# A decoder trunk on one core: down projections with the high and low activations side by side in one 512-column matmul

## The chip, the core and the metric

The kernel runs on one core of one Trainium2 chip. The metric is the device time of one execution in microseconds, as the median of several runs. The engines of the core have the profile's names here: PE is TensorE (matmuls, with PEld for the loads of its stationary weights), DVE is VectorE, ACT is ScalarE, POOL is GpSimd and SP is SyncE, which issues the transfers of the weights.

## What is computed

The reference is a decoder trunk of two layers on 256 tokens of 1024 features. Layer 0 mixes tokens with a recurrent block, layer 1 with sparse attention. A squared-ReLU MLP of width 4096 follows each mixer. The change touches the second product of that MLP, `w_down`, and the residual addition behind it.

```python
def _sq_relu_mlp(h, w_up, w_down):
    u = jax.nn.relu(h @ w_up)
    return (u * u) @ w_down

for i in range(DEPTH):
    h = _rmsnorm(x, norm_mix[i])
    x = x + mixer(h)
    h = _rmsnorm(x, norm_ffn[i])
    x = x + _sq_relu_mlp(h, mlp_w_up[i], mlp_w_down[i])
return _rmsnorm(x, norm_final)
```

## The kernel before

Everything is held transposed: a tile has 128 features on the partitions and the 256 tokens (S) along its free dimension. The residual stream `xt` is eight such chunks, and an output chunk m of a product is one accumulation in a PSUM bank, 128 partitions by 256 tokens, a half of the bank's 512 float32 columns.

The products need more precision than one pass of TensorE's reduced float32 (`F32R`) gives. So each operand is split into a high part, rounded to that format, and a low part, the difference. A product is then three matmuls for each 128-row slice k: high weights by high activations, high weights by low activations, low weights by high activations. `mm3` (lines 317 to 320) issues them in this order, and each brings a load of its own stationary weight tile, 128 by 128:

```python
pe.matmul(ps, wh, xh, start=start, stop=False)
pe.matmul(ps, wh, xl, start=False, stop=False)
pe.matmul(ps, wl, xh, start=False, stop=stop)
```

`start` clears the bank, and the matmuls behind it add to it until `stop`. The high weights come from ACT (line 278, tile `whi`), the low ones from DVE (line 287, `wlo`), both from a raw tile that SP loads (line 264). There are seven buffers of each, and `tick` (line 300) keeps the splitting up to six pieces ahead of the product that uses them. One piece is 128 by 1024: eight slices k.

The MLP is the function `mlp` (line 766). It first runs 32 up projections, whose results are squared and split on DVE and ACT (lines 778 to 785) into 32 tiles `uhl`. Such a tile is 512 columns wide, the high part `uh` in its first half and the low part `ul` in its second:

```python
uhl = [up.tile([P, 2 * S], F32R, name="uhl", tag="uhl", bufs=NF) for _ in range(NF)]
uh, ul = [x[:, :S] for x in uhl], [x[:, S:] for x in uhl]
zrot = rotation(3, 4, 5, 0, 1, 2)
```

Then come the down projections (lines 797 to 817): eight output chunks m, each of four pieces j with eight slices k, so 32 slices and 96 matmuls a chunk. The banks go round a rotation of six. At the end of a chunk `residual` (line 521) adds the bank to `xt` on DVE, and an epilogue follows: in layer 0 the scaled copies for the next mixer (`chunk_h`, `hhl`) and the squares for the norm, in layer 1 the scaling by the final norm. The eighth chunk of layer 1 is another case (`seeded`): the residual is put into the bank by two identity matmuls ahead of it, and `finish` takes the result from the bank.

What runs in which order in the MLP is the order of the code. The two sections around it (recurrent block and attention) are ordered by a planner, which is given a duration and the needs of each piece of work; its tables are not changed.

Of the kernel before, what the change touches and what calls it, by code (L numbers as in the profile page):

```python
# [20 lines left out]
S = 256  # L21
D = 1024
KC = D // P
NF = 32
# [195 lines left out]
def trunk_kernel(ctx: ExitStack, tc: tile.TileContext, x_in, vec_in, const_in, w2_in, wts, out):  # L220
    nc = tc.nc
    ctx.enter_context(tc.manual_schedule())
    pe, dve, act, pool = nc.tensor, nc.vector, nc.scalar, nc.gpsimd
# [12 lines left out]
    def rotation(*ids):  # L236
        while True:
            for i in ids:
                yield bank(i)
# [52 lines left out]
    def later(fn):  # L292
        deferred.append(fn)

    def flush():
        todo, deferred[:] = deferred[:], []
        for fn in todo:
            fn()

    def tick(lo=None, hi=None, n=1):  # L300
        for i in range(max(n, 1)):
            more = n and state["split"] - state["get"] < LOOK
            if more:
                split_lo(lo)
            if i == 0:
                flush()
            if more:
                split_hi(hi)

    def get(name, idx):  # L310
        i = state["get"]
        assert order[i] == (name, idx), (order[i], name, idx)
        state["get"] += 1
        assert state["lo"] > i
        return hi_t[i % NSPL], lo_t[i % NSPL]

    def mm3(ps, wh, wl, xh, xl, start, stop):
        pe.matmul(ps, wh, xh, start=start, stop=False)  # L318
        pe.matmul(ps, wh, xl, start=False, stop=False)  # L319
        pe.matmul(ps, wl, xh, start=False, stop=stop)  # L320

    def diff(o, a, h):
        return lambda e: e.tensor_tensor(o, a, h.bitcast(F32), op=OP.subtract)  # L323
# [9 lines left out]
    class Section:  # L333
# [55 lines left out]
        def proj(self, name, idx, b, t, step, xs=None, xk=None):  # L389
            wh, wl, wk = self.weight(name, idx, t)  # L390
            z = self.bank((name, idx), b, zcols)
            xs, xk = xs or [(hh[:, k], hl[:, k]) for k in range(KC)], xk or hkey
            for i in range(0, 4, self.join):
                ks = range(2 * i, 2 * (i + self.join))

                def run(e, ks=ks):
                    for k in ks:
                        w = slice(k * P, (k + 1) * P)
                        mm3(z(), wh[:, w], wl[:, w], xs[k][0], xs[k][1], k == 0, k == KC - 1)
                self.add("pe", 0.68 * self.join, run, r=wk + list(xk[ks.start:ks.stop]), w=[("ps", b)], t=t + i * step)  # L400
            return z, ("ps", b)
# [119 lines left out]
    def residual(z, m):  # L521
        dve.tensor_tensor(xt[:, m], xt[:, m], z, op=OP.add)  # L522


    with ExitStack() as ph:
# [45 lines left out]
        for k in range(KC):  # L571
# [6 lines left out]
                w=[("hh", k)], t=t)  # L578
# [3 lines left out]
        for q in range(4):  # L582
            for i in range(NFINE):
                w = slice(256 * q, 256 * q + 256)
# [6 lines left out]
        for a, b, n in ((0, 2, 2), (0, 1, 1), (4, 6, 2), (4, 5, 1), (0, 4, 1)):  # L591
            add("dve", 0.07 + 0.267 * n, lambda e, a=a, b=b, n=n: e.tensor_tensor(
                x2[:, a:a + n], x2[:, a:a + n], x2[:, b:b + n], op=OP.add), r=[("x2", b + i) for i in range(n)],
                w=[("x2", a + i) for i in range(n)], t=4 + a / 4)
# [43 lines left out]
        zb = {"n": 0}  # L638
# [5 lines left out]
        def conv(m, t):  # L644
            b = nextbank()
            if m < NFINE:
                wh, wl, _ = sec.weight("in", 8 + m, t)
                z, zk = sec.bank(("in", 8 + m), b, zcols), ("ps", b)
                for k in range(KC):
                    def run(e, k=k):  # L650
                        w = slice(k * P, (k + 1) * P)
                        mm3(z(), wh[:, w], wl[:, w], hh[:, k], hl[:, k], k == 0, k == KC - 1)
                        if m == 0 and k == 1:
                            keep_warm(8)
                    add("pe", 0.323 + 0.9 * (m == 0 and k == 1), run, r=[("hi0", m, k // 2), ("lo0", m, k // 2), ("hi", m), ("lo", m), hkey[k]],
                        w=[zk], t=m * 0.33 + k * NI * PJ / 2 if m < NI else t + k * PJ / 2)
            else:
                z, zk = sec.proj("in", 8 + m, b, t, PJ)
            t += 4 * PJ
            x, xk = xps[m % 3], ("xp", m % 3)  # L660
            bk = ("xb", m)
            add("dve", 0.34, lambda e: e.tensor_tensor(x[:, 3:], z(), rs, op=OP.mult), r=[zk, "rs"], w=[xk], t=t)
            add("act", 0.49, lambda e: e.activation(xb[m], x[:, 3:], AF.Identity, bias=col(V_CB, m), scale=cw(3, m)),
                r=[xk], w=[bk], t=t)
            for i in range(3):
                add("dve", 0.4, lambda e, i=i: e.scalar_tensor_tensor(xb[m], x[:, i:i + S], cw(i, m), xb[m], op0=OP.mult,
                                                                      op1=OP.add), r=[xk], w=[bk], t=t)
# [82 lines left out]
        for m in range(8):  # L750
            wh, wl, wk = sec.weight("out", m, to + 2.65 * m)
            b = nextbank()
            z = sec.bank(("out", m), b, zcols)
            for i in range(4):
                def run(e, i=i, z=z, wh=wh, wl=wl):
                    for k in (2 * i, 2 * i + 1):
                        w = slice(k * P, (k + 1) * P)
                        mm3(z(), wh[:, w], wl[:, w], xbh[k], xbl[k], k == 0, k == KC - 1)
                add("pe", 0.68, run, r=wk + pk[2 * i] + pk[2 * i + 1], w=[("ps", b)], t=to + 2.65 * m + i * PJ)
            t = to + 2.65 * (m + 1)  # L760
            add("dve", 0.34, lambda e, z=z, m=m: residual(z(), m), r=[("ps", b)], w=[("xt", m)], t=t)
            sec.norm(m, V_GF, t)
# [3 lines left out]
    def mlp(layer, epilogue, first, last=None):  # L766
        with ExitStack() as ph:
            up = ph.enter_context(tc.tile_pool(name="up%d" % layer, bufs=1, side="right"))
            tmp = ph.enter_context(tc.tile_pool(name="mtmp%d" % layer, bufs=2))
            if last:  # L770
                xh, xl, ir = (tmp.tile([P, n], F32R, name=a, bufs=1) for a, n in (("xh", S), ("xl", S), ("ir", P)))
# [4 lines that stand above are left out]
            def up_post(m, z):  # L776
                t = tmp.tile([P, S], F32, name="t", tag="t")
                dve.scalar_tensor_tensor(t, z, 0.0, rs, op0=OP.max, op1=OP.mult)  # L778
                flush()
                if m >= len(first) - 1:  # L780
                    tick(n=2 if m < 16 else 1)
                u = tmp.tile([P, S], F32, name="u", tag="u")
                act.activation(u, t, AF.Square)  # L783
                act.activation(uh[m], t, AF.Square)  # L784
                later(lambda: dve.tensor_tensor(ul[m], u, uh[m].bitcast(F32), op=OP.subtract))  # L785

            for m in range(NF):
                if m >= len(first):
                    z = next(zrot)[:, :S]
                    wh, wl = get("up%d" % layer, m)  # L790
                    for k in range(KC):
                        w = slice(k * P, (k + 1) * P)
                        mm3(z, wh[:, w], wl[:, w], hh[:, k], hl[:, k], k == 0, k == KC - 1)
                else:
                    z = first[m]()
                up_post(m, z)
            for m in range(8):
                z = next(zrot)[:, :S]
                seeded = last is not None and m == 7
                if last and m == 6:  # L800
                    act.copy(ir, ident)
                    act.copy(xh, xt[:, 7])
                    diff(xl, xt[:, 7], xh)(dve)
                if seeded:
                    pe.matmul(z, ir, xh, start=True, stop=False)
                    pe.matmul(z, ir, xl, start=False, stop=False)
                for j in range(4):
                    wh, wl = get("dn%d" % layer, m * 4 + j)
                    for k in range(8):
                        w, i = slice(k * P, (k + 1) * P), j * 8 + k  # L810
                        mm3(z, wh[:, w], wl[:, w], uh[i], ul[i], i == 0 and not seeded, i == NF - 1)
                    if j == 3 and seeded:
                        last(z)
                    elif j == 3:
                        residual(z, m)
                        epilogue(m)
                    tick()

    def to_mix(m):
        chunk_h(m, V_GM, m < KC - 1)  # L820
        chunk_stats(m)

    mlp(0, to_mix, up0)


    with ExitStack() as ph:
# [36 lines left out]
        for i in range(2):  # L863
            o = offs[-1] + (4 + i) * P * 1024
            add("sp", 1.5, lambda e, i=i, o=o: e.dma_start(w1[i], wts[o:o + P * 1024].rearrange("(p n) -> p n", p=P)),
                w=[("w1", i), "loads"] + w1k, t=-12, lag=2.0)
# [544 lines left out]
```

## Time and profile before

| | |
|---|---|
| median of 3 runs | 568.36 us (568.14 to 568.47) |
| profiled execution, span from first to last instruction | 566.4 us |
| up projections of layer 0 end, down projections of layer 0 begin | 174.3 us |
| first matmul of the attention section | 261.5 us |
| down projections of layer 1, first seven chunks | 470.8 to 546.9 us |
| eighth chunk, to its last matmul | to 558.0 us |
| VectorE busy from 174.3 to 261.5 us | 48.97 us |
| ScalarE busy from 174.3 to 261.5 us | 34.56 us |
| PEclk from 174.3 to 261.5 us | 1.00 |

A row of the groups gives source line, engine, operation, the tiles written and read, the shapes, the count, the busy time and the mean duration of one. Behind the second bar stands how long the engine was idle just ahead of it, and what ended that. A row of the timeline gives the start in us, the duration in us, the engine, the line and the operation. Matmuls overlap: the duration of one reaches from its start through the array to the bank, and the next one starts long before that. What a matmul costs in a stream is the interval between two starts.

### The profile page before, as it was taken

How to read it: one execution, taken by the hardware profiler on the slowest of the kernel's cores; microseconds unless marked ns; L12 is line 12 of the kernel's file. 1: busy time of each engine (PE TensorE's matmuls, PEld its weight loads, DVE VectorE, ACT ScalarE, POOL GpSimd, SP SyncE). 2: the span in 40 equal slices, each digit the busy share in tenths (PEclk: the TensorE clock that was granted, in tenths of full speed). 3: DMA queues.
4: the chain of work that ended last, by engine and by line, in shares of the span. 5: the costliest groups of instructions: out<-in, count | busy, mean ns of one | idle time of the engine just before them, and what ended most of it. 6: DMA issues, size and time to landing. Idle time of an engine off the chain costs nothing.

```text
span 566.4 us, 12406 instructions
## 1 busy us (share of the span) xinstructions
PE 559.3 (99%) x4902; PEld 552.9 (98%) x4902; DVE 407.6 (72%) x873; ACT 343.9 (61%) x670; POOL 40.1 (7%) x55
## 2 busy tenths in 40 slices
PE   9999999999999999999999999999999999999995
PEld 9989999999999999999999999999999999999995
DVE  6899989776676565466839999999767775563532
ACT  7699675866564443354647999875855664443421
POOL 1000000000000121131000000000000000222310
PEclk9999999999999999999999999999999999999998
DMA  8936467566667456555765431264766667566402
GB/s 319 407 91 220 117 219 247 176 204 192 188 192 249 155 189 217 190 181 175 276 188 166 140 99 57 75 224 138 221 200 192 196 200 233 154 202 221 132 1 74
DMA packets 33225, 103.66 MB, mean 183 GB/s; under 512 B 3856, under 2 KB 8080, under 8 KB 33168
## 3 DMA queue, kind: packets, MB, share of 16 engines
q1 hardware_dynamic: 32624, 102.42, 56.1%
q8 instruction: 38, 0.62, 0.5%
q10 hardware_dynamic: 544, 0.46, 0.2%
q14 instruction: 19, 0.16, 0.1%
HBM read 99.23 MB, written 1.05 MB: 177 GB/s over the span
## 4 chain that ended last, share of the span: by engine, by line
PE 99%; DVE 0%; ACT 0%; DVEq 0%; POOL 0%; issue 0%; POOLq 0%
PE bank L318 28%; PE bank L319 28%; PE bank L320 28%; PE bank L1177 3%; PE bank L686 2%; PE bank L1159 2%; PE bank L1105 1%; PE bank L1106 1%; PE bank L567 1%; PE bank L1012 1%; PE bank L1013 1%; PE bank L1014 1%; PE bank L953 1%; DVE xg L1295 0%; PE bank L1287 0%; DVEq L1406 0%
## 5 line engine op out<-in xcount | busy, mean ns | idle before, releaser
L318 PE MATMUL bank<-hhl,whi 128*128 128x256 f32 x768 | 213.1, 278 | 0.0
L319 PE MATMUL bank<-hhl,whi 128*128 128x256 f32 x768 | 212.4, 277 | 0.0
L320 PE MATMUL bank<-hhl,wlo 128*128 128x256 f32 x768 | 212.3, 276 | 0.0
L318 PEld LDWEIGHTS bank<-hhl,whi 128*128 128x128 f32 x768 | 144.5, 188 | 0.1
L287 DVE TENSOR_TENSOR wlo<-raw,whi 128x1024 fp32r<-128x1024 f32 x115 | 143.2, 1266 | 1.9 <-ACT whi L278 1.9
L319 PEld LDWEIGHTS bank<-hhl,whi 128*128 128x128 f32 x768 | 144.5, 188 | 0.1
L320 PEld LDWEIGHTS bank<-hhl,wlo 128*128 128x128 f32 x768 | 144.4, 188 | 0.0
L319 PE MATMUL bank<-uhl,whi 128*128 128x256 f32 x512 | 141.4, 276 | 0.0
L320 PE MATMUL bank<-uhl,wlo 128*128 128x256 f32 x512 | 141.3, 276 | 0.0
L318 PE MATMUL bank<-uhl,whi 128*128 128x256 f32 x512 | 141.3, 276 | 0.0
L278 ACT CAST whi<-raw 128x1024 fp32r<-128x1024 f32 x116 | 118.1, 1039 | 23.1 <-issue 18.8
L318 PEld LDWEIGHTS bank<-uhl,whi 128*128 128x128 f32 x512 | 96.1, 188 | 0.0
L320 PEld LDWEIGHTS bank<-uhl,wlo 128*128 128x128 f32 x512 | 96.1, 188 | 0.0
L319 PEld LDWEIGHTS bank<-uhl,whi 128*128 128x128 f32 x512 | 96.1, 188 | 0.0
L323 DVE TENSOR_TENSOR wlo<-raw,whi 128x1024 fp32r<-128x1024 f32 (+2 forms) x72 | 77.1, 1089 | 2.9 <-ACT whi L326 2.8
L326 ACT CAST whi<-raw 128x1024 fp32r<-128x1024 f32 (+2 forms) x64 | 61.2, 969 | 16.8 <-PE bank L319 7.8
L522 DVE TENSOR_TENSOR xt<-xt,bank 128x256 f32<-128x256 f32 x39 | 15.9, 417 | 74.8 <-PE bank L320 74.5
L783 ACT ACTIVATE u<-t 128x256 f32<-128x256 f32 x64 | 26.7, 418 | 58.6 <-DVE t L778 57.2
L778 DVE SCALAR_TENSOR_TENSOR t<-bank,rstd 128x256 f32<-128x256 f32 x64 | 26.9, 423 | 41.0 <-PE bank L320 40.7
L1119 ACT ACTIVATE pt<-pt,mx 128x128 f32<-128x128 f32 (+1 forms) x64 | 28.6, 450 | 1.8 <-DVE mx L1116 1.4
L785 DVE TENSOR_TENSOR uhl<-u,uhl 128x256 fp32r<-128x256 f32 x64 | 26.6, 416 | 3.0 <-ACT uhl L784 3.0
L498 ACT ACTIVATE hhl<-xt,vec 128x256 fp32r<-128x256 f32 x8 | 4.1, 510 | 39.4 <-DVE xt L522 39.4
(202 smaller groups left out, 732.6 us busy)
## 6 DMA issues: line engine op xcount, KB each, us to landing
raw<-in_dram SPq DMA_DIRECT2D x171, 512.0 KB, 4.4
raw<-in_dram SPq DMA_DIRECT2D x4, 560.0 KB, 4.6
gw<-in_dram SPq DMA_DIRECT2D x4, 512.0 KB, 8.9
raw<-in_dram SPq DMA_DIRECT2D x6, 256.0 KB, 4.9
y<-in_dram SPq DMA_DIRECT2D x2, 512.0 KB, 7.4
pT<-in_dram SPq DMA_DIRECT2D x2, 512.0 KB, 5.4
xt<-in_dram SPq DMA_DIRECT2D x3, 256.0 KB, 4.9
kl<-tl SPq DMA_DIRECT2D x8, 64.0 KB, 4.0
```

What stands on the lines that cost most here:

```text
L278: (act.copy if eng is None else eng.tensor_copy)(hi_t[i % NSPL][:, :n], raw_of(i)[:, :n])
L287: (eng or dve).tensor_tensor(lo[:, :n], raw_of(i)[:, :n], hi[:, :n].bitcast(F32), op=OP.subtract)
L318: pe.matmul(ps, wh, xh, start=start, stop=False)
L319: pe.matmul(ps, wh, xl, start=False, stop=False)
L320: pe.matmul(ps, wl, xh, start=False, stop=stop)
L323: return lambda e: e.tensor_tensor(o, a, h.bitcast(F32), op=OP.subtract)
L326: return lambda e: (e.copy if e is act else e.tensor_copy)(o, a)
L778: dve.scalar_tensor_tensor(t, z, 0.0, rs, op0=OP.max, op1=OP.mult)
L783: act.activation(u, t, AF.Square)
L785: later(lambda: dve.tensor_tensor(ul[m], u, uh[m].bitcast(F32), op=OP.subtract))
L1119: add("act", (0.39, 0.49)[qc], lambda e, row=row, j=j: e.activation(row, row, AF.Exp, bias=mx[:, j:j + 1], scale=-1.0, accum_out=sm[:, j:j ...
L1177: two = lambda c, w, y, **k: [e.matmul(o()[own_(hf), c0 + c.start:c0 + c.stop], w(hf), y(hf), **k) for hf in range(2)]
```

## The change

A new helper `mm2` takes the place of `mm3` in all down projections but the eighth chunk of layer 1. It moves the whole `uhl` tile, 512 columns, against one load of the high weights, and writes a whole bank: the first half gets high by high, the second half high by low. Then it moves the high activations against the low weights into the second half. So there are two accumulations side by side in one bank, and `residual` is called twice at a chunk's end, once for each half.

```diff
+    def mm2(ps, wh, wl, xhl, start, stop):
+        pe.matmul(ps, wh, xhl, start=start, stop=False)
+        pe.matmul(ps[:, S:], wl, xhl[:, :S], start=False, stop=stop)
...
             for m in range(8):
-                z = next(zrot)[:, :S]
+                zf = next(zrot)
+                z, zb = zf[:, :S], zf[:, S:]
...
-                        mm3(z, wh[:, w], wl[:, w], uh[i], ul[i], i == 0 and not seeded, i == NF - 1)
+                        if seeded:
+                            mm3(z, wh[:, w], wl[:, w], uh[i], ul[i], False, i == NF - 1)
+                        else:
+                            mm2(zf, wh[:, w], wl[:, w], uhl[i], i == 0, i == NF - 1)
                     if j == 3 and seeded:
                         last(z)
                     elif j == 3:
                         residual(z, m)
+                        residual(zb, m)
                         epilogue(m)
```

Four lines are added ahead of everything else, so a line of the old kernel behind 320 has a number higher by four or more in the new one; the two matmuls of `mm2` are lines 323 and 324, and `residual` is line 526.

In PE's order, where layer 0's down projections begin (`bank` is the PSUM bank, `hhl` the last up projection's activations, `whi` and `wlo` the weight pieces), before:

```order
L320 MATMUL bank_2275<-hhl,wlo_96 128x256
L318 MATMUL bank_2309<-uhl,whi_83 128x256
L319 MATMUL bank_2309<-uhl,whi_83 128x256
L320 MATMUL bank_2309<-uhl,wlo_90 128x256
L318 MATMUL bank_2309<-uhl,whi_83 128x256
```

and in the changed kernel, from the same place:

```order
L320 MATMUL bank_2275<-hhl,wlo_96 128x256
L323 MATMUL bank_2309<-uhl,whi_83 128x512
L324 MATMUL bank_2309<-uhl,wlo_90 128x256
L323 MATMUL bank_2309<-uhl,whi_83 128x512
L324 MATMUL bank_2309<-uhl,wlo_90 128x256
```

Of the three matmuls of a slice, two have become one of twice the width; over the kernel PE has 480 matmuls less.

In DVE's order, at the end of layer 0's first chunk (`raw` is a loaded piece, `xt` the residual stream), before:

```order
L287 TENSOR_TENSOR wlo_90<-raw_79,whi_83 128x1024
L522 TENSOR_TENSOR xt<-xt,bank_2309 128x256
L287 TENSOR_TENSOR wlo_91<-raw_80,whi_84 128x1024
L501 SCALAR_TENSOR_TENSOR hhl<-xt,vec,hhl 128x256
L287 TENSOR_TENSOR wlo_92<-raw_81,whi_85 128x1024
```

and in the changed kernel:

```order
L287 TENSOR_TENSOR wlo_90<-raw_79,whi_83 128x1024
L526 TENSOR_TENSOR xt<-xt,bank_2309 128x256 x2
L287 TENSOR_TENSOR wlo_91<-raw_80,whi_84 128x1024
L505 SCALAR_TENSOR_TENSOR hhl<-xt,vec,hhl 128x256
L287 TENSOR_TENSOR wlo_92<-raw_81,whi_85 128x1024
```

One addition has become two in a row; all else on DVE, and all of ACT, POOL and SP, stands as before.

The end of layer 0's last chunk is followed by the first projections of the attention section, which use the scaled copies `hhl` slice by slice. In PE's order (here with the buffers' numbers and the engines waited for) the last slice comes late in that sequence, behind parts of three chunks, in the kernel before:

```order
L320 MATMUL bank2_3317<-hhl_106,wlo6_96 128x256
L318 MATMUL bank0_3269<-hhl_106,whi4_87 128x256
L319 MATMUL bank0_3269<-hhl_106,whi4_87 128x256
L320 MATMUL bank0_3269<-hhl_106,wlo4_94 128x256
L318 MATMUL bank0_3269<-hhl_106,whi4_87 128x256 [waits Activation_49]
L319 MATMUL bank0_3269<-hhl_106,whi4_87 128x256 [waits DVE_49]
```

Nothing moved there: the changed kernel has the same rows at this place, 45 matmuls behind the section's first in both.

## The prediction

> **What bounds the kernel now.** I read the page first: the shares of the engines, then the chain that ended last, then the costliest groups.
>
> ```profile
> span 566.4 us, 12406 instructions
> PE 559.3 (99%) x4902; PEld 552.9 (98%) x4902; DVE 407.6 (72%) x873; ACT 343.9 (61%) x670; POOL 40.1 (7%) x55
> PE 99%; DVE 0%; ACT 0%; DVEq 0%; POOL 0%; issue 0%; POOLq 0%
> L318 PE MATMUL bank<-uhl,whi 128*128 128x256 f32 x512 | 141.3, 276 | 0.0
> ```
>
> The chain is TensorE from end to end, and PE never waits before the down projections' matmuls (idle 0.0). So the time is the sum of the intervals from one matmul's start to the next. The 276 ns of a group's row is no such interval: it is a latency, and 512 of them three times over would be far more than the two stages last. The interval comes from starts, so I asked for the instructions on the tile uhl, once for layer 0's down projections and once for the first seven chunks of layer 1's (the eighth is not changed).
>
> ```profile
> L318 PE MATMUL bank<-uhl,whi x256: 276/276/280, 174.3 to 261.2; 128*128 128x256 f32 x128
> L318 PE MATMUL bank<-uhl,whi x224: 276/276/281, 470.8 to 546.6; 128*128 128x256 f32 x112
> ```
>
> Between the first and the last L318 lie 255 steps in 86.9 us (340.8 ns) and 223 steps in 75.8 us (339.9 ns). A step is the three matmuls of one 128-row slice k, so **one step costs 340.4 ns**, 113.5 ns a matmul, and the change touches 256 + 224 = 480 steps, 163.4 us of the span. One ns on a step is 0.48 us.
>
> **The change part by part.** Removed: in each of 480 steps the second load of the same high weight tile and one matmul instruction. Kept: the columns that move, 3 x 256 before, 512 + 256 now. So nothing is computed less; what can be won or lost is what a matmul costs beside its columns. No matmul of 512 columns stands in the trace, and its price decides everything. I look for rows that separate a part for each matmul from a part for each column.
>
> First, the stream as it is, in the timeline near the end of layer 1's seventh chunk:
>
> ```profile
> 545.14 0.28 PE L320 MATMUL bank<-uhl,wlo 128*128 128x256 f32 x1
> 545.25 0.28 PE L318 MATMUL bank<-uhl,whi 128*128 128x256 f32 x1
> ...
> 546.84 0.28 PE L320 MATMUL bank<-uhl,wlo 128*128 128x256 f32 x1
> ```
>
> From 545.14 to 546.84 there are 15 matmuls: 113.3 ns each. But the same matmuls, with the same tiles, also run at another pace. At the start of layer 0's down projections:
>
> ```profile
> 174.56 0.28 PE L320 MATMUL bank<-uhl,wlo 128*128 128x256 f32 x1
> 174.68 0.28 PE L318 MATMUL bank<-uhl,whi 128*128 128x256 f32 x1
> ...
> 177.06 0.28 PE L320 MATMUL bank<-uhl,wlo 128*128 128x256 f32 x1
> ```
>
> Here 21 matmuls take 2.50 us, 119 ns each. So 256 columns have **two paces**, 113.3 and about 118 to 119, and the fast one is what the kernel has nearly all the time. Now the only long stretch in which reduced-precision matmuls of different lengths follow each other, three of 304 columns and three of 256 in turn (the value projections, also with a weight load each):
>
> ```profile
> 280.12 0.30 PE L1012 MATMUL bank<-whi,hhl 128*128 128x304 f32 x1
> 280.26 0.30 PE L1013 MATMUL bank<-wlo,hhl 128*128 128x304 f32 x1
> 280.39 0.30 PE L1014 MATMUL bank<-whi,hhl 128*128 128x304 f32 x1
> 280.53 0.28 PE L1012 MATMUL bank<-whi,hhl 128*128 128x256 f32 x1
> 280.65 0.28 PE L1013 MATMUL bank<-wlo,hhl 128*128 128x256 f32 x1
> 280.77 0.28 PE L1014 MATMUL bank<-whi,hhl 128*128 128x256 f32 x1
> 280.89 0.30 PE L1012 MATMUL bank<-whi,hhl 128*128 128x304 f32 x1
> ...
> 283.20 0.30 PE L1012 MATMUL bank<-whi,hhl 128*128 128x304 f32 x1
> ```
>
> Four rounds take 3.08 us, 770 ns a round of 1680 columns; in the first round three matmuls of 256 take 0.36 us and three of 304 take 0.41. I put 118 ns on the 256 and so 770/3 - 118 = 138.7 on the 304. The fast pace does not come back in these four rounds: a length that differs from the one before keeps the stream in the slow pace. Third, what a column costs at most when nothing else does:
>
> ```profile
> L686 PE MATMUL bank<-xb,gw x64: 378/379/380, 29.5 to 43.8; 128*128 128x256 f32 x64
> 29.48 13.11 PE L686 MATMUL bank<-xb,gw 128*128 128x256 f32 x60
> ```
>
> These are full-precision matmuls (32 calls in the code, 64 instructions). Sixty in a row last 13.11 us, of which the last one's latency is 0.38, so 59 intervals of 215.8 ns. If that is two passes over 256 columns, a column costs at most 215.8/512 = 0.42 ns.
>
> **The sum.** A matmul of 512 columns is a 304 with 208 more: 138.7 + 208 x 0.42 = 226 ns. The 256 behind it I take at the slow pace, 118, since it follows a longer one as in the value projections. A step is then 344 ns against 340.4, +3.6 ns, times 480 = **+1.7 us**. In words: two matmuls that each carry about 11 ns beside their columns against three that carry 113.3 - 256 x 0.42 = 6. The ends of the range for the 512: 215.8 (the row that lasts nearest to it, without any extra) and 512 x 770/1680 = 234.7 (all of a round's time put on columns). For the 256: 113.3 and 119. I choose values near the 304, since it is the longest single-pass matmul that the trace has.
>
> **A rule against this forecast.** The row first: 138.7 ns for 304 columns, with a load of the next weights beside it. The Trainium skill, page "TensorE: Matmul & The Clock Gate", section "Step-by-step: what each phase is for", says that the next weights come through a read port of their own and take no bandwidth from the matmul that runs, and its section "Back-to-back issue gap" gives an isolated matmul N/2.4 + 2.5 ns. By that a 512 would be 215.8 and a 256 would be 109.2, an estimate of 325.0 ns a step and -7.4 us. The trace agrees for the full-precision row (215.8) and not for the reduced-precision ones: 113.3 and 118 for 256, and 138.7 where the formula has 129.2 for 304. That the measured excess comes from the load beside the matmul is my guess; no row shows it.
>
> **What lies beside other work.** VectorE gets 8 + 7 = 15 additions more:
>
> ```profile
> L522 DVE TENSOR_TENSOR xt<-xt,bank 128x256 f32<-128x256 f32 x7 | 3.0, 421 | 33.6 <-PE bank L320 33.6
> ```
>
> This is the answer by lines for 184 to 254 us. Each takes 421 ns, 6.3 us in all, but VectorE stood idle 33.6 us in seven waits for the chunk's last matmul, 4.8 us a chunk, and the weight tiles that it makes are fetched up to six pieces ahead. So the additions cost nothing; were that cover gone, at most 15 x 0.42 = 6.3 us. Behind the second addition queue the next low weight tile on VectorE and, on ScalarE, the scaled copy hhl and the casts. At the end of layer 0 this is tightest:
>
> ```profile
> 262.69 0.48 DVE L501 SCALAR_TENSOR_TENSOR hhl<-xt,vec,hhl 128x256 fp32r<-128x256 f32 x1 [0.58 <-ACT hhl L498]
> 265.45 0.42 DVE L323 TENSOR_TENSOR accl<-acc,acch 128x256 fp32r<-128x256 f32 x1 [0.47 <-ACT acch L326]
> 266.61 0.28 PE L318 MATMUL bank<-hhl,whi 128*128 128x256 f32 x1
> ```
>
> The last slice of hhl is ready at 263.17 and first used by the k = 7 matmuls of the next projection, whose first is the row at 266.61 (the one with the waits in PE's order above). 3.4 us of slack take a delay of 0.42. The order of VectorE is otherwise unchanged, and no DMA or queue is moved. The eighth chunk of layer 1 keeps its three matmuls; if it starts in the slow pace and never leaves it, 96 x 5.7 = 0.5 us more, which I leave to the range. The kernel's tail behind it is untouched.
>
> The sum is made on the profiled execution: 566.4 + 1.7 = 568.1 us of span. The median of the runs, 568.36, is 2.0 above that span, so the forecast is **570.1 us**.
>
> **The rivals.**
> - A, the extra falls with the count: each matmul keeps the fast pace's 6 ns, so the 512 takes 113.3 + 256 x 0.42 = 220.8 and the 256 takes 113.3; 334.1 a step, -3.0 us, 565.3. For it: the mean step of 340.4 ns is within 0.4 of three times 113.3, so nearly all steps run at this pace now. Against it: the pace is lost wherever lengths differ. This is the case on the other side; it decides at a 512 of 340.4 - 118 = 222 ns if the 256 is slow, 227 if it is fast.
> - B, a long matmul has no extra at all, as the rule above has it: 215.8 + 113.3 = 329.1, -5.4 us, 562.9. For it the full-precision row, against it the 304.
> - C, the slow 512 with a fast 256: 226 + 113.3 = 339.3, -0.5 us, 567.8, no change that can be told. For it: a long matmul gives the load behind it all the time it needs, so the pace could come back in each step. Against it: the 256s behind the 304s stay at 118.
> - D, the extra is a column's, not a matmul's: 770/1680 = 0.458 ns for 768 columns and 352 a step, +5.6 us, 573.9, or 574.4 with the eighth chunk slow too. For it: 118/256 = 0.461 and 138.7/304 = 0.456 are equal within the rounding. Against it: the same columns at 113.3.
> - That the change does not do what it says is excluded: PE's order has the 512 and the 256 in each step.
>
> **How the numbers follow.** The forecast 0.33 (its own range 569.0 to 572.0), A 0.22, B 0.11, C 0.21, D 0.13. D alone is left out of the range, which goes from B's 562.9 to 573.0, between the forecast and D. About 0.2% (1.1 us) is what a measurement of this kernel can tell from no change: faster is A and B, 0.33; the same is C, 0.21; slower is the forecast and D, 0.46.
>
> **What would show it.** In the changed kernel's trace the step from one 512 to the next is 344 ns, the 512 holds PE for 226 and the 256 for 118; the values stage and the up projections keep their intervals; the residual additions start in pairs with VectorE's wait ahead of the first about 0.4 us shorter; PE stays at idle 0.0. A step under 338 ns makes the forecast wrong by A or B, one over 350 by D, and a wait of PE for VectorE ahead of 266.6 us would break the part on hidden work.

## The result and the profile after

The changed kernel takes **574.0 us** (median of 4 runs, 573.77 to 574.53) against 568.41 (4 runs, 568.14 to 568.50): a ratio of 1.0102 with a 95% interval of 1.0088 to 1.0116. It is slower by about 5.6 us, where 1.7 were forecast, and the time lies above the range. The profiled execution's span went from 566.4 to 572.4 us. The page of the changed kernel begins like this (span; busy time, share and count of each engine; further down the shares of the chain that ended last, and the two groups of new matmuls):

```profile
span 572.4 us, 11456 instructions
PE 564.9 (99%) x4422; PEld 537.3 (94%) x4422; DVE 414.0 (72%) x888; ACT 343.6 (60%) x670; POOL 40.0 (7%) x55
...
PE 96%; DVE 1%; DMA 1%; ACT 1%; issue 0%; DVEq 0%; POOL 0%; POOLq 0%
...
L323 PE MATMUL bank<-uhl,whi 128*128 128x512 f32 x480 | 167.9, 394 | 0.0
L324 PE MATMUL bank<-uhl,wlo 128*128 128x256 f32 x480 | 134.8, 281 | 0.0
```

PE has 480 matmuls and 480 loads fewer and is busy for 5.6 us longer. Ahead of the new matmuls it never waits (0.0), so what the down projections lost lies in the intervals. The chain is no longer PE alone: VectorE, transfers and ScalarE hold about 1% each. The answers for the tile uhl give the count and the first and last start, for layer 0 and for layer 1's seven chunks:

```profile
L323 PE MATMUL bank<-uhl,whi x256: 388/392/397, 174.5 to 263.6; 128*128 128x512 f32 x128
...
L323 PE MATMUL bank<-uhl,whi x224: 391/392/397, 474.6 to 552.5; 128*128 128x512 f32 x112
```

255 steps in 89.1 us and 223 in 77.9 us: **349.4 ns a step**, where the kernel before had 340.4 and the forecast 344. Inside a step, PE's timeline (start, duration, engine, line):

```profile
199.64 0.39 PE L323 MATMUL bank<-uhl,whi 128*128 128x512 f32 x1
199.87 0.28 PE L324 MATMUL bank<-uhl,wlo 128*128 128x256 f32 x1
199.99 0.39 PE L323 MATMUL bank<-uhl,whi 128*128 128x512 f32 x1
```

The 512 holds PE for 0.23 us, the 256 behind it for 0.12. Taken from the starts of all 480 steps, the means are **230.8 ns for the 512 and 118.7 for the 256**, together 349.5. The other engines and the clock do not explain it. The table of stretches (span; busy us and count of PE, PEld, DVE, ACT, POOL; granted clock, DMA share, GB/s), first of the kernel before, then of the changed one:

```profile
190.00:250.00 60.00, 60.00 (x532) 60.00 (x531) 32.60 (x32) 23.05 (x26) 11.68 (x10) 1.00 0.61 199
```

```profile
190.00:250.00 60.00, 60.00 (x346) 52.67 (x345) 35.50 (x37) 23.16 (x27) 11.70 (x10) 1.00 0.57 193
```

The clock is 1.00 in both, and the transfers move no more than before. The 512s that ran while VectorE was idle throughout (about 190 of them) and those that ran while it was busy throughout (about 257) have the same mean interval, 230.9 ns.

So (349.5 - 340.3) x 480 = 4.4 us of the 6.0 us of span come from the steps. Most of the rest, 1.4 us, is in the section between the two layers' down projections: its length from the first matmul behind layer 0's last step to layer 1's first is 210.6 us against 209.3. The first such loss is a wait that the kernel before does not have. The chain of waits around 270 us:

```profile
269.45 0.13 PE bank L320
...
269.62 1.15 DVE wlo L327 x2
270.76 0.33 issue
271.09 2.55 DVE wlo L327 x2
273.64 1.67 DVE rstd L435
```

For 6 us the chain runs over VectorE: it makes four low weight tiles and then, with no gap between them, the reciprocal of the attention norm, on which PE waits.

### The profile page after: what moved, and what is told of

Same layout as the page of the kernel before. It is cut to its first block, busy times and chain, and to the rows that moved or that the text cites. A ratio compares the mean times of both kernels' runs of the same rounds, so it can differ in the third digit from the quotient of the medians.

```text
span 572.4 us, 11456 instructions
## 1 busy us (share of the span) xinstructions
PE 564.9 (99%) x4422; PEld 537.3 (94%) x4422; DVE 414.0 (72%) x888; ACT 343.6 (60%) x670; POOL 40.0 (7%) x55
## 4 chain that ended last, share of the span: by engine, by line
PE 96%; DVE 1%; DMA 1%; ACT 1%; issue 0%; DVEq 0%; POOL 0%; POOLq 0%
PE bank L323 19%; PE bank L318 18%; PE bank L319 18%; PE bank L320 18%; PE bank L324 10%; PE bank L690 2%; PE bank L1186 2%; PE bank L1168 2%; PE bank L1114 1%; PE bank L1115 1%; PE bank L571 1%; PE bank L1021 1%; DMA raw<-in_dram 1%; PE bank L1022 1%; PE bank L1023 1%; DVE wlo L327 1%
## 5 line engine op out<-in xcount | busy, mean ns | idle before, releaser
L323 PE MATMUL bank<-uhl,whi 128*128 128x512 f32 x480 | 167.9, 394 | 0.0
L324 PE MATMUL bank<-uhl,wlo 128*128 128x256 f32 x480 | 134.8, 281 | 0.0
L323 PEld LDWEIGHTS bank<-uhl,whi 128*128 128x128 f32 x480 | 90.4, 188 | 20.4
L324 PEld LDWEIGHTS bank<-uhl,wlo 128*128 128x128 f32 x480 | 90.3, 188 | 0.0
L526 DVE TENSOR_TENSOR xt<-xt,bank 128x256 f32<-128x256 f32 x54 | 22.3, 419 | 73.9 <-PE bank L324 71.3
L1279 ACT ACTIVATE xg<-xt,vec 128x256 f32<-128x256 f32 x7 | 3.6, 511 | 40.6 <-DVE xt L526 40.6
L496 POOL TENSOR_TENSOR acc<-xt 128x256 f32<-128x256 f32 x2 | 2.9, 1466 | 337.1 <-DVE xt L526 183.6
```

The source lines that it names most:

```text
L323: pe.matmul(ps, wh, xhl, start=start, stop=False)
L324: pe.matmul(ps[:, S:], wl, xhl[:, :S], start=False, stop=stop)
```

## The experiments

Five questions were open: do the halves and the second additions cost anything without a 512; does a change of length from one matmul to the next make the pace slow; is it the load; is it the reduced-precision type; and which of the 15 additions costs time.

**Two halves instead of the 512.** Same banks, same 15 additions, three matmuls of 256:

```diff
-        pe.matmul(ps, wh, xhl, start=start, stop=False)
+        pe.matmul(ps[:, :S], wh, xhl[:, :S], start=start, stop=False)
+        pe.matmul(ps[:, S:], wh, xhl[:, S:], start=False, stop=False)
```

> Back to three matmuls of 256 columns a step, with the bank in two halves and the two residual additions of the change kept. My theory (the whole loss in the down projections is the matmuls' pace): a step is back at 340.4 ns, and against the kernel before only the second addition is left, 0.4 to 0.9 us where VectorE's queue ends at TensorE behind layer 0's last chunk: 568.9 to 569.3 us. Rival (the two halves of a bank, or the added reads of it, slow TensorE): the step stays near 349.5 ns and the time near 574.

Measured: 569.29 us (11 runs) against 568.35, ratio 1.0016 (1.0008 to 1.0025). PE's timeline in layer 0's second to third chunk, first and last of 25 starts of the line:

```profile
197.73 0.28 PE L323 MATMUL bank<-uhl,whi 128*128 128x256 f32 x1
...
205.89 0.28 PE L323 MATMUL bank<-uhl,whi 128*128 128x256 f32 x1
```

24 steps in 8.16 us: 340.0 ns. The step is that of the kernel before, so the whole loss in the steps, that of the 256 behind the 512 too, comes with the 512. About 0.9 us remain without it.

**Runs of equal lengths.** In each piece first the eight 512s, then the eight 256s:

```diff
-                            mm2(zf, wh[:, w], wl[:, w], uhl[i], i == 0, i == NF - 1)
+                            pe.matmul(zf, wh[:, w], uhl[i], start=i == 0, stop=False)
+                    for k in range(0 if seeded else 8):
+                        w, i = slice(k * P, (k + 1) * P), j * 8 + k
+                        pe.matmul(zb, wl[:, w], uh[i], start=False, stop=i == NF - 1)
```

> The eight 512-column matmuls of a piece first, then its eight 256-column ones: the same matmuls, one change of length in eight. Theory that lengths in turn lose the fast pace: inside a run of 256 the pace comes back, 113.3 ns, and inside a run of 512 it falls to 220; 334 to 338 ns for a 512 and a 256, time 565 to 567. Theory that a 512 costs what it costs and only a 256 behind a 256 can be fast: 230.8 + 113.9 = 344.7, time 571.7. Theory that the slow pace, once there, stays until a wait of TensorE resets it: 349.5, time 574.

Measured: 574.71 us (4 runs), ratio 1.0108 (1.0092 to 1.0123), no better than the changed kernel. PE's timeline, where a row holds a whole run of eight:

```profile
197.24 2.02 PE L819 MATMUL bank<-uhl,whi 128*128 128x512 f32 x8
199.10 1.10 PE L822 MATMUL bank<-uhl,wlo 128*128 128x256 f32 x8
200.05 2.00 PE L819 MATMUL bank<-uhl,whi 128*128 128x512 f32 x8
```

Eight 512s take 1.86 us to the next row's start, 232 each; eight 256s take 0.95 us, 119 each. Seven of eight follow a matmul of their own length and are slow all the same. That the length changes from one matmul to the next is therefore not the condition.

**Both matmuls with 512 columns.** The low weights move the whole tile too, which adds the product of low by low:

```diff
-        pe.matmul(ps[:, S:], wl, xhl[:, :S], start=False, stop=stop)
+        pe.matmul(ps, wl, xhl, start=False, stop=stop)
```

> Both weight tiles move 512 columns, so low by low is computed too (256 columns more a step). All lengths in the down projections are equal. Theory that lengths in turn lose the fast pace: two times 220 = 440 ns a step. Theory that a 512 has no fast pace (the fast pace belongs to 256 columns, where the load of 128 weights lasts as long as the matmul): two times 230.8 = 461.6 ns a step; the span then grows by 480 x (461.6 - 349.5) = 53.8 us against the changed kernel.

Measured: 628.73 us (one run). First and last of 40 matmuls in a row:

```profile
197.63 0.40 PE L323 MATMUL bank<-uhl,whi 128*128 128x512 f32 x1
...
206.71 0.40 PE L324 MATMUL bank<-uhl,wlo 128*128 128x512 f32 x1
```

39 intervals in 9.08 us, 232.8 ns; over all of them 231.5. A uniform stream of 512s has the same price as the 512 of the pair: it is the 512's own, not that of its neighbour.

**One matmul of 272 among 256s.** In 30 of a chunk's 32 steps:

```diff
+        pe.matmul(ps[:, :S], wh, xhl[:, :S], start=False, stop=False)
+        pe.matmul(ps[:, S - 16:], wh, xhl[:, S - 16:], start=False, stop=False)
+        pe.matmul(ps[:, S:], wl, xhl[:, :S], start=False, stop=stop)
```

> Three loads a step again, of 256, 272 and 256 columns; 16 columns of each step are computed twice and land where they do not belong. Theory that lengths in turn lose the fast pace: 118.7 + 125.6 + 118.7 = 363 ns a step. Theory that each matmul has its own pace whatever stands beside it, and only lengths over 256 are slow: 113.3 + 125.6 + 113.3 = 352. If the fast pace is had by all: 113.3 + 120 + 113.3 = 347.

Measured: 580.11 us (one run); first and last of 25 starts:

```profile
198.18 0.28 PE L327 MATMUL bank<-uhl,whi 128*128 128x256 f32 x1
...
206.92 0.28 PE L327 MATMUL bank<-uhl,whi 128*128 128x256 f32 x1
```

24 steps in 8.74 us, 364 a step; over all steps the 256s hold PE for 119.8 and 118.7 ns and the 272 for 124.9. Sixteen columns in one matmul of three make all three slow. A chunk's first step has a 512 here as well, but that alone does not explain it: all 15 changed chunks are slow, and with the same first step and 256s alone, in a run further below, 7 of 15 are fast.

**All three with 272.**

```diff
+        pe.matmul(ps[:, :S + 16], wh, xhl[:, :S + 16], start=False, stop=False)
+        pe.matmul(ps[:, S - 16:], wh, xhl[:, S - 16:], start=False, stop=False)
+        pe.matmul(ps[:, S - 16:], wl, xhl[:, :S + 16], start=False, stop=stop)
```

> Three loads a step with 272 columns each (30 of the 32 steps of a chunk; the 16 columns more are computed twice and land where they do not belong). All lengths are equal, and none is 256. If equal lengths have a fast pace of their own: 120 ns each, 360 a step. If the fast pace belongs to 256 columns against 128 weights alone and every other length follows 6.6 ns + 0.438 ns a column: 125.7 each, 377 a step.

Measured: 587.01 us (one run); first and last of 20 starts:

```profile
198.75 0.28 PE L327 MATMUL bank<-uhl,whi 128*128 128x272 f32 x1
...
205.94 0.29 PE L327 MATMUL bank<-uhl,whi 128*128 128x272 f32 x1
```

19 steps in 7.19 us, 378 a step, 126 a matmul. At 0.443 ns a column, the fast 256's price (113.3 / 256), a 272 would be 120.4. Equal lengths alone do not bring the fast pace either.

**Half the load.** The pair with 64 weight columns in place of 128:

```diff
+        pe.matmul(ps[:64], wh[:, :64], xhl, start=False, stop=False)
+        pe.matmul(ps[:64, S:], wl[:, :64], xhl[:, :S], start=False, stop=stop)
```

> The changed kernel's step with weight tiles of 64 columns in 30 of 32 steps (the lower half of the product is left out), so each load is half as long. Theory that the load beside a matmul slows its columns: the excess over the fastest column price (0.4167 ns) falls by about half, 512 from 230.8 to about 222 and 256 from 118.7 to about 113, a step of 335. Theory that the load has no part in it: 349.5 as before.

Measured: 574.25 us (one run). The answer for uhl on PEld shows that the load is shorter, in the stretch from 197.8 to 206.8 us; the second fence, PE's timeline, shows the first and last of 27 starts:

```profile
L327 PEld LDWEIGHTS bank<-uhl,whi x26: 133/134/136, 197.8 to 206.6; 128*64 128x64 f32 x26
```

```profile
197.57 0.39 PE L327 MATMUL bank<-uhl,whi 128*64 128x512 f32 x1
...
206.67 0.39 PE L327 MATMUL bank<-uhl,whi 128*64 128x512 f32 x1
```

A load lasts 134 ns instead of the 188 that the changed kernel's page gives, and the step stays at 9.10 us / 26 = 350 ns. The prediction's guess that the excess comes from the load beside the matmul does not hold, so far as the load's length would show it.

**Half the load with three 256s.**

```diff
+        pe.matmul(ps[:64, :S], wh[:, :64], xhl[:, :S], start=False, stop=False)
+        pe.matmul(ps[:64, S:], wh[:, :64], xhl[:, S:], start=False, stop=False)
+        pe.matmul(ps[:64, S:], wl[:, :64], xhl[:, :S], start=False, stop=stop)
```

> Three matmuls of 256 columns a step with weight tiles of 64 columns in 30 of 32 steps (the lower half of the product is left out). Theory that the fast pace of 113.3 ns is set by the load of 128 weights, each matmul starting when its load ends: with a load half as long the matmul is bound by its own columns, so either faster than 113.3 (about 109 to 112, if the load's time was all that held it) or at the slow pace of 118 (if the fast pace needs that lockstep). Theory that 113.3 is the matmul's own time: unchanged, 340 a step.

Measured: 572.79 us (one run). Two stretches of PE's timeline, first and last start of the same line in each:

```profile
187.03 0.28 PE L327 MATMUL bank<-uhl,whi 128*64 128x256 f32 x1
...
193.74 0.28 PE L327 MATMUL bank<-uhl,whi 128*64 128x256 f32 x1
...
199.00 0.28 PE L327 MATMUL bank<-uhl,whi 128*64 128x256 f32 x1
...
205.80 0.28 PE L327 MATMUL bank<-uhl,whi 128*64 128x256 f32 x1
```

57 intervals in 6.71 us are 117.7 ns, 60 in 6.80 us are 113.3. It is the same code, chunk by chunk: by the starts, 7 of the 15 changed chunks run at 113.3 from the end of their first third at the latest, 8 run at 117.5 to 117.9 throughout, and none changes later. So there are two paces, each lasts over some 90 matmuls here, and which one a chunk gets is settled near its start. With full loads and 256s alone the slow pace did not last: in the kernel before and in the two halves, layer 0's first chunk starts at 119 and is at 113.3 before half of it has run, and the other chunks of the down projections run at 113.3. Whether it is the half load or the 512 in a chunk's first step that lets the slow pace last here is not separated.

**Another type.** The operands read as bf16, the upper half of each word, in the same places:

```diff
+        ws, xs = [t.bitcast(BF16)[:, 1::2] for t in (wh, wl)], xhl.bitcast(BF16)[:, 1::2]
+        pe.matmul(ps, ws[0], xs, start=False, stop=False)
+        pe.matmul(ps[:, S:], ws[1], xs[:, :S], start=False, stop=stop)
```

> The changed kernel, but in 30 of a chunk's 32 steps the 512 and the 256 read the upper half of each word of the same tiles as bf16, in the same places (every second bf16 element), instead of the whole word in reduced-precision fp32; the low parts of the products are lost in these steps. Theory 'a column of the reduced-precision type costs 0.438 ns': the excess goes with the type, the 512 comes near 2 x 108 = 216 ns and the 256 to 108-113, a step of 324-330 against 349.5, and 450 steps bring 9 to 11 us: 563-565 us. Rival 'a column costs 0.438 ns in any single-pass stream of 512 and 256 with loads': 231 and 118.7 stay, 574 us. Second rival, the stride of four bytes halves the rate: a step of 650 or more, over 700 us.

Measured: 570.92 us (one run, 568.02 before). First and last of 28 starts:

```profile
197.54 0.39 PE L329 MATMUL bank<-uhl,whi 128*128 128x512 bf16 x1
...
206.72 0.39 PE L329 MATMUL bank<-uhl,whi 128*128 128x512 bf16 x1
```

27 steps in 9.18 us: **340.0 ns, to a tenth the step of three 256s**. The 512 holds PE for 226 ns, twice 113.3. Both numbers expected were missed: the slow pace is gone with the type, but the 512 does not come down to 216. The change of type also changes what is read, two bytes of every four, and no run separates the two. The time stays 2.9 us above the kernel before all the same. In the profiles the section between the two layers' down projections is 1.6 us longer than before, with the delays that are taken up further below, and the down projections themselves 0.4 us.

> The kernel with the 512 in two halves of 256, as in e1_halves, and in 30 of a chunk's 32 steps the three matmuls read the upper half of each word as bf16, as in e9_bf16_pair (the low parts of the products are lost). Theory 'the fast pace is the weight load's own, 110.0 ns behind its start and 3.3 to the next': 113.3 a matmul and 340 a step as in e1_halves, 569.3 us, though the columns alone would take less. Rival 'the fast pace is what 256 columns of the reduced-precision type cost': 256 columns in bf16 run at 108-110, a step of 324-330, 562-565 us.

The same with the 512 in two halves. Measured: 569.46 us (one run); first and last of 24 starts:

```profile
198.01 0.27 PE L329 MATMUL bank<-uhl,whi 128*128 128x256 bf16 x1
...
205.83 0.27 PE L329 MATMUL bank<-uhl,whi 128*128 128x256 bf16 x1
```

23 steps in 7.82 us, 340.0 again. The number is the one expected if the load set the fast pace, but the run before speaks against that reason: behind a 512 the load has twice the time, and the 512 still costs exactly two 256s. As far as these two lengths show, the fast pace is a price of columns: 113.3 / 256 = 0.443 ns.

**The last addition.** The two halves as above, but layer 0's eighth chunk in the old form with one addition (14 additions more instead of 15; layer 1's eighth is old in all kernels):

```diff
-                        if seeded:
-                            mm3(z, wh[:, w], wl[:, w], uh[i], ul[i], False, i == NF - 1)
+                        if m == 7:
+                            mm3(z, wh[:, w], wl[:, w], uh[i], ul[i], i == 0 and not seeded, i == NF - 1)
...
-                        residual(zb, m)
+                        if m < 7:
+                            residual(zb, m)
```

> As the kernel with three matmuls in two halves and two additions, but the last chunk of layer 0 in the old form with one addition. Theory that of the 15 additions only the one behind layer 0's last chunk costs time: back at the time of the kernel before, 568.3 to 568.6 us. Rival (the additions cost where they stand, 0.06 us each): 569.2 us.

Measured: 568.54 us (11 runs) against 568.39, ratio 1.0003 (0.9994 to 1.0012): no loss that can be told. Of the 0.9 us of the two halves, 0.75 are gone (the two intervals just overlap). VectorE's timeline shows the place; first the kernel before, then the changed one, the two halves, and this kernel:

```profile
261.70 0.42 DVE L522 TENSOR_TENSOR xt<-xt,bank 128x256 f32<-128x256 f32 x1 [4.61 <-PE bank L320]
...
270.73 1.74 DVE L431 RECIPROCAL rstd<-rstd 128x256 f32<-128x256 f32 x1
```

```profile
264.16 0.88 DVE L526 TENSOR_TENSOR xt<-xt,bank 128x256 f32<-128x256 f32 x2 [4.47 <-PE bank L324]
...
268.72 4.92 DVE L327 TENSOR_TENSOR wlo<-raw,whi 128x1024 fp32r<-128x1024 f32 x4
273.56 1.75 DVE L435 RECIPROCAL rstd<-rstd 128x256 f32<-128x256 f32 x1
```

```profile
261.51 0.87 DVE L527 TENSOR_TENSOR xt<-xt,bank 128x256 f32<-128x256 f32 x2 [4.16 <-PE bank L325]
...
270.91 1.74 DVE L436 RECIPROCAL rstd<-rstd 128x256 f32<-128x256 f32 x1
```

```profile
261.07 0.42 DVE L527 TENSOR_TENSOR xt<-xt,bank 128x256 f32<-128x256 f32 x1 [4.15 <-PE bank L320]
...
270.10 1.75 DVE L436 RECIPROCAL rstd<-rstd 128x256 f32<-128x256 f32 x1
```

From the addition's start to the reciprocal's it is 9.03 us before, 9.40 with two additions, 9.40 in the two halves, and 9.03 again here. PE's timeline shows who waits, first in the kernel before, then in the two halves:

```profile
272.74 0.28 PE L966 MATMUL bank<-cst,rstd 1*128 1x1 f32 x2
272.99 0.39 PE L318 MATMUL bank<-hhl,whi 128*128 128x256 f32 x1
```

```profile
273.17 0.39 PE L318 MATMUL bank<-hhl,whi 128*128 128x256 f32 x1 [0.18 <-DVE tt L946]
```

By starts, the two gaps around PE's two small matmuls on rstd are 0.36 and 0.37 us in the two halves, against 0.21 and 0.16 before and 0.21 and 0.16 again in this kernel. In all ten kernels with that addition the matmul behind them comes 0.36 to 0.37 us late.

## Why the prediction was wrong, by its steps

**What bounds the kernel:** right. PE's intervals set the time before and after, and PE stays at idle 0.0 ahead of the new matmuls.

**The slow pace of the pair:** right in its effect, wrong in its condition. The 256 costs 118.7 ns as forecast (118). But "a length that differs from the one before keeps the stream in the slow pace" is not the rule: runs of eight equal lengths, and streams of 272 or 512 alone, are slow too, and a uniform stream of 256 with half loads is found in both paces.

**The term that failed: T512 = 138.7 + 208 x 0.42 = 226.** The measured 512 is 230.8. These 4.8 ns, and 0.7 on the 256, times 480 are 2.6 us, and make +4.3 us of the forecast's +1.7. The step was read as two matmuls that each carry about 11 ns beside their columns, against three that carry 6. The 0.42 ns a column came from full-precision matmuls, in which two passes over 256 columns were assumed; it is not the price of a column in these streams. At the fast pace a 256 and, in bf16, a 512 cost 113.3 and 226, so a column costs 0.443 and a matmul carries next to nothing beside its columns. So there was nothing to win by merging: 768 columns cost 340 ns in three matmuls of either type and in two of bf16. What can be lost is the pace: against the fast price, the slow 256 has 5.4 ns more (118.7 - 113.3) and the slow 512 4.2 (230.8 - 2 x 113.3). 3 x 113.3 + 5.4 + 4.2 = 349.5, the step that was measured.

The Trainium skill, page "TensorE: Matmul & The Clock Gate", section "Back-to-back issue gap", gives a formula for an isolated matmul, by which the prediction's estimate for a 512 and a 256 together was 325 ns. The runs do not agree for either type: 349.5 in reduced float32, and 340.0 in bf16.

**The rivals.** A and B (a fixed extra that is saved, or none at all) are excluded by the 512 alone. C's step, 226 + 113.3, is to within a nanosecond what the pair does in bf16; in reduced float32 the pace never came back. D (the extra is a column's) was nearest with 352 and 573.9 us. That its time is so close is luck: its step is 2.5 ns too long, 1.2 us in all, and the section between the layers, which it leaves out, adds 1.4. But it should have had more weight than 0.13: 118/256 and 138.7/304 were quoted as equal and then set aside for a column price from another kind of matmul. Its mechanism fits in the fast pace, where all of the price is a column's; the slow pace adds a part for each matmul, and so 349.5 came out below 352.

**"So the additions cost nothing":** right for 14 of 15 as far as the times can tell, wrong for the one behind layer 0's last chunk. The slack that was checked, 3.4 us from hhl to its first use, was not the tightest. From the copy accl to the reciprocal VectorE has no gap, and the added 0.42 us moves all of that work by 0.37. In the changed kernel PE's small matmuls on rstd come 0.15 us later and the one behind them 0.37; some 30 matmuls further on, which start in the slow pace behind the wait, it is 0.51. Half a microsecond of the result is this, and the run without that addition takes it away.

**The rest of the section:** three more delays, none of them tested by itself. +0.23 us at 282 us stands behind the small transfer from tt to pt; it appears in the four kernels whose step is a 512 and a 256 (+0.08 to +0.85) and in none of the other seven. +0.15 at 349 us appears in all ten kernels with the addition behind layer 0's last chunk and not in the one without it, so it is likely to hang on that addition too. +0.45 at 379 us stands behind a weight piece: ScalarE waits 2.45 us for its landing, and the rounding of oh, VectorE's ol and PE come behind that in turn. It also appears in the kernel of the last experiment (+0.35) but hardly in the two halves (+0.09), so it comes and goes. The profiled start of the kernel adds 0.15 us; over all these kernels that start differs by 1.2.

**The eighth chunk:** the 0.5 us that were left to the range did not come. It starts at 117 ns a matmul and is at 113.3 before half of it has run.

What stays open is why the pair in reduced float32 never falls into the fast pace and in bf16 always does. The runs exclude as the sole reason the length of the load, the neighbour's length, VectorE's traffic and, since the 512 in bf16 does it too, that one matmul writes a whole bank. They settle nothing beyond that.

## What to carry to other kernels

Before merging two matmuls that share weights, find out whether a matmul carries anything beside its columns in that stream, from two lengths of the same type at the same pace; where it does not, there is nothing to gain, and a steady pace can be lost. A price taken from another type of matmul is not the price of a column. A small operation on an engine that has slack on average can cost nearly its full time (here 0.37 us of 0.42) where that engine has a queue without gaps ahead of something that the critical engine awaits: look for that place at the end of each stage.

## What the runs showed of the hardware

- A stream of reduced-precision float32 matmuls of 256 columns has two paces, 113.3 and 117.5 to 119 ns, at the same clock of 1.00. With weights of 64 columns each lasted for whole chunks of some 90 matmuls; with 128 columns, and 256s alone, the slow one was left within half a chunk.
- Lengths of 272 and 512 in reduced float32 ran in these streams only near 125 and 231 ns, uniform or mixed. The uniform 272s take 126, with a longer interval of 134 at every third one in long stretches, which is not explained.
- In bf16, read in place with a step of two elements, 256 and 512 columns cost 113.3 and 226 to 227 ns: no less than reduced float32 at its fast pace.
- Half as many weight columns shorten a load's record from 188 to 134 ns and leave the pair's step at 350 ns.
